# Attention scores as half-height matmuls: both components side by side in the array, three products each, one PSUM tile

## The chip, the cores and the metric

The kernel runs on one core of one Trainium2 chip. A core has a matrix engine (TensorE, "PE" in the profile), three others that compute (VectorE "DVE", ScalarE "ACT", GpSimd "POOL") and a queue engine (SyncE, "SP") that here issues nearly all DMAs. TensorE multiplies a stationary operand of up to 128 rows by 128 columns, loaded by a separate instruction ("PEld"), with a moving operand of up to 512 columns, and adds up in PSUM, a memory of eight banks of 512 float32 values per partition. The metric is the time of one execution on the device in microseconds (us).

## The reference

A decoder block of 2048 positions and 1024 channels: a normalised input is projected, one branch is a gated linear recurrence, the other a differential attention; both are gated, merged, projected and added to the input. The change is in the attention. Each of the 8 heads has two components (`c`) of 64 channels; each component gives scores and a softmax of its own, and the difference of the two, with a factor, weights the values.

```python
HEAD_DIM = D_MODEL // (2 * N_HEADS)          # 64
...
for qb in range(S // Q_BLOCK):               # 16 blocks of 128 queries
    ...
    s = jnp.einsum('bqhcd,bkhcd->bhcqk', q[:, q0:q1], k[:, :q1]).astype(jnp.float32) * scale
    ...
    p = jax.nn.softmax(s, axis=-1)
    w = p[:, :, 0] - lam * p[:, :, 1]
    outs.append(jnp.einsum('bhqk,bkhe->bqhe', w.astype(v.dtype), v[:, :q1]))
```

## The kernel before

**Numbers as pairs.** Nearly every float32 operand of a matmul is kept as a pair of float16 tiles, a high part and a low part (the rest). A product of two pairs is mostly taken as three matmuls, high x high, high x low and low x high.

**Stages.** From the start to about 468 us the recurrence branch runs. From 468 to about 1945 us runs the attention stage, in which the change lies. After it come the branch projections, the merge and the output projection.

**Attention units.** A unit is one head and 128 queries (`u.h`, `u.t`), 8 x 16 = 128 units in all. Unit t has t + 1 key blocks of 128 keys. `pieces(t)` (line 796) divides them into a first piece of at most eight blocks and, from t = 8 on, a second with the rest. `a_scores(u, ci)` (line 800) makes the scores of component `ci`, piece by piece: for each piece a PSUM tile `sc` of two banks (1024 columns) from the pool `ps_s` with two buffers (line 592), matmuls for each chunk of 512 keys (line 814), then VectorE copies the scores into an SBUF tile `e0` (component 0) or `e1` (component 1) and takes the row maximum (line 826), with the causal mask on the last block (line 830). The pool of `e0` and `e1` has four buffers each.

**The stacking before.** Component `ci` has 64 channels, half of the array's rows. K is therefore stored as `[128, 2, 512]`: for each component the high part on partitions 0 to 63 and the low part on 64 to 127. Q is stored twice per component, once high over low (`v = 0`) and once low over high (`v = 1`). Two matmuls over all 128 rows then give all four products:

```python
for v in range(2):
    nc.tensor.matmul(ps[:, x * 128:x * 128 + m], Qt[h, t // 4][:, v, ci, q0:q0 + 128],
                     K[:, ci, 0:m], start=(v == 0), stop=(v == 1))
```

**How K and Q get there.** The projections `g_k` and `g_q` (lines 672 and 685) make 128 channels of a head for 512 positions, component 0 on partitions 0 to 63 and component 1 on 64 to 127, by 24 matmuls (`mm3`, line 192). `split16` (line 665) writes the high part with ScalarE (line 667) and the low part with VectorE (line 668) into a tile `st`; DMAs on SP then move the halves into place, four for K (lines 680 and 681) and six for Q (lines 693 to 695). They are put off (`later`) until the next projection group has been issued.

**The rest of a unit.** `a_exp` (line 837) applies the exponential on ScalarE (line 851). `a_comb` (line 854) combines both components on VectorE (line 874), takes the high part on ScalarE (876) and the low part on GpSimd (877), and transposes both by DMA (880) into `pt`. `a_pv` (line 886) multiplies with v (line 897).

**Order.** The string `ORD = "0fc1eFp"` gives the order within a unit: the scores of component 0 ("0"), one group of projections ("f"), the combination of the unit before ("c"), the scores of component 1 ("1"), the exponentials ("e"), the other projection groups that are due ("F"), and the product with v of two units earlier ("p"). Projection groups are those for k, q, v with its gate (`g_va`, line 711) and the merge gates (`g_gm`). A planner of the framework may move instructions of an engine from this order when their inputs or buffers would not be ready.

Of the kernel before, what the change touches and what calls it, by code (L numbers as in the profile page):

```python
# [24 lines left out]
CH = 512  # L25
NC = S // CH
HALF = 1024
EPS = 1e-6
GM_T = 8   # groups of gate projections kept for the end of the attention
LAG = 2    # units between a unit's scores and its product with v  # L30
ACC0 = 8.0  # projection groups ahead of the attention units
PD = 5     # x tiles loaded ahead
# order in an attention unit: scores (0, 1), exponentials (e), combination of the unit before (c),
# product with v of an earlier one (p), with projection groups between them (f: one, F: all that are due)
ORD = "0fc1eFp"
SEG_A = 2  # where a head's gate projections stand between its chunks
SEG_B = 5
# [6 lines left out]
def p2(e):  # L44
    return float(2.0 ** e)
# [3 lines left out]
def kernel(  # L49
# [44 lines left out]
    with ExitStack():  # L94
# [33 lines left out]

# [1 line left out]
        class W:  # L130
            pass

        def w16_at(i):
            """one of the four places for a block of weights"""
            return lambda w: w16_p.tile([128, 2, KD, 128], F16, tag=f"w{i % 4}", name="w16")
# [24 lines left out]
        def w_scale(w, ps, fac, keep=None):  # L160
            """power of two that brings the block's norm close to 2^13 (a rough sum is enough for it)"""
            nc.tensor.matmul(ps[:, 0:1], ones16, w.ss, start=True, stop=True)
            tot = tl(1, "w_tot")
            nc.vector.tensor_scalar(out=tot, in0=ps[:, 0:1], scalar1=1e-30, scalar2=None, op0=ALU.max)
            w.sg, w.iv = keep or (tl(1, f"w_sg_{w.tag}"), tl(1, f"w_iv_{w.tag}"))
            pow2_bits(w.sg, tot, 13)
            pow2_inv(w.iv, w.sg)
            if keep is None:
                w.cz = wn_p.tile([128, 1], F32, tag=f"w_cz_{w.tag}", name="w_cz",
                                 bufs={"wg": 4, "agm": 3}.get(w.tag, 2))  # L170
                nc.vector.scalar_tensor_tensor(out=w.cz, in0=w.iv, scalar=fac, in1=cu, op0=ALU.mult, op1=ALU.mult)
# [9 lines left out]

# [1 line left out]
        utx = ExitStack()  # L183
# [3 lines left out]
        def mm3(ps, w, c0, n):  # L187
            """ps[f128, n] += w^T u over all of d, s in [c0, c0 + n)"""
            i = 0
            for k in range(KD):  # L190
                for a, b in ((0, 0), (0, 1), (1, 0)):
                    nc.tensor.matmul(ps, w.t[:, a, k, :], uT[:, b, k, c0:c0 + n],  # L192
                                     start=(i == 0), stop=(i == 3 * KD - 1))
                    i += 1

        # ================= RG-LRU branch =================
        with ExitStack() as lx:
# [21 lines left out]
            def prep_g(gr):  # L219
                """power of two that keeps the scaled, normalised input in fp16's range"""  # L220
                ss, tot = tl(1, "g_ss"), tl(1, "w_tot")
# [56 lines left out]

            # weight pipeline
            order = [(C_XR if i % 2 == 0 else C_ZR) + (i // 2) * 128 for i in range(2 * KD)]  # L280
# [16 lines left out]
            def in_half(b, hf, z, w):  # L297
                """PSUM tile of a half row of an x_r (z = 0) or z_r (z = 1) block"""
                if hf == 0 and 2 * b + z < 3:
# [142 lines left out]
            x_fin(4, 2, gb)  # L442
            # per-channel vectors: rows of 128 channels, turned into columns
            rows = le.tile([65, 128], F32, tag="rows", bufs=1, name="rows")
# [24 lines left out]
            with tc.issue_after(x_last[1]):  # L469
                # block-diagonal gate weights, exact f32r hi/lo  # L470
                gf_t = []
# [13 lines left out]
            with after_x():  # L485
                nc.vector.tensor_scalar(out=ba, in0=ba, scalar1=0.5, scalar2=None, op0=ALU.mult)
                nc.vector.tensor_scalar(out=bx, in0=bx, scalar1=0.5, scalar2=None, op0=ALU.mult)
                # softplus(-a) = max(-a, 0) + log1p(exp(-|a|)), log1p(t) = 2 atanh(t / (2 + t))
                spm, spe, sps, spq, spr = (lc.tile([128, KD], F32, name=f"sp{i}") for i in range(5))
# [85 lines left out]

        # ================= differential attention and merge gates =================
        QT = S // 128
        wfac_a = cst.tile([128, KD], F32, name="wfac_a")
        ya_ss = cst.tile([128, NH * NC], F32, name="ya_ss")
        with ExitStack() as ax:  # L580
# [10 lines left out]
            t4 = ax.enter_context(tc.tile_pool(name="t4", bufs=6))  # L591
            ps_s = ax.enter_context(tc.tile_pool(name="ps_s", bufs=2, space=PSUM))
            ps_o = ax.enter_context(tc.tile_pool(name="ps_o", bufs=2, space=PSUM))
            ps_m = ax.enter_context(tc.tile_pool(name="ps_m", bufs=2, space=PSUM))

# [1 line left out]
            wl = {k: ws[2 * KD + i] for i, k in enumerate(ahead)}  # L597
# [16 lines left out]
            def wadv(n):  # L614
                """weight blocks up to index n ready; two more on their way"""
                while wpos[0] < min(n + 3, len(worder)) or wpos[1] < min(n + 2, len(worder)) or wpos[2] < min(n + 1, len(worder)):
# [38 lines left out]

# [1 line left out]
            Kt, Qt, Vt, Gt = {}, {}, {}, {}  # L657
# [6 lines left out]

            def split16(ps):
                st = sp.tile([128, 2, CH], F16, tag="st", name="st")
                nc.scalar.activation(st[:, 0], ps, AF.Copy, scale=p2(-14))
                nc.vector.scalar_tensor_tensor(out=st[:, 1], in0=ps, scalar=p2(-14), in1=st[:, 0],  # L668
                                               op0=ALU.mult, op1=ALU.subtract)
                return st  # L670

            def g_k(h, c):
                ps = ps_m.tile([128, CH], F32, tag="mm", name="mm")
                mm3(ps, wl["k", h], c * CH, CH)
                st = split16(ps)
                t = kp.tile([128, 2, CH], F16, tag="K", name="K")

                def mv():
                    for i in range(2):
                        nc.sync.dma_start(out=t[0:64, i, :], in_=st[64 * i:64 * i + 64, 0, :])  # L680
                        nc.sync.dma_start(out=t[64:128, i, :], in_=st[64 * i:64 * i + 64, 1, :])
                later.append(mv)
                Kt[h, c] = t

            def g_q(h, c):
                ps = ps_m.tile([128, CH], F32, tag="mm", name="mm")
                mm3(ps, wl["q", h], c * CH, CH)
                st = split16(ps)
                t = qp.tile([128, 2, 2, CH], F16, tag="Q", name="Q")

                def mv():
                    for i in range(2):
                        nc.sync.dma_start(out=t[0:64, :, i, :], in_=st[64 * i:64 * i + 64, :, :])
                        nc.sync.dma_start(out=t[64:128, 0, i, :], in_=st[64 * i:64 * i + 64, 1, :])
                        nc.sync.dma_start(out=t[64:128, 1, i, :], in_=st[64 * i:64 * i + 64, 0, :])
                later.append(mv)
                Qt[h, c] = t
# [93 lines left out]

# [1 line left out]
            class U:  # L793
# [5 lines left out]

            def a_scores(u, ci):  # L800
                h, t = u.h, u.t
                if ci == 0:
                    u.n = 1 if t == 0 else (2 if t <= 8 else 3)
                    u.mx = t4.tile([128, 2, 3], F32, tag="mx", name="mx")
                    u.e = {}
                col = 0
                for pi, (b0, nb) in enumerate(pieces(t)):
                    ps = ps_s.tile([128, 1024], F32, tag="sc", name="sc")
                    for x in range(0, nb, 4):
                        m = min(4, nb - x) * 128  # L810
                        K = Kt[h, (b0 + x) // 4]
                        q0 = (t % 4) * 128
                        for v in range(2):
                            nc.tensor.matmul(ps[:, x * 128:x * 128 + m], Qt[h, t // 4][:, v, ci, q0:q0 + 128],  # L814
                                             K[:, ci, 0:m], start=(v == 0), stop=(v == 1))
                    if ci == 0:
# [5 lines left out]
                    u.e[ci, pi] = (e, ev)  # L822
                    last = b0 + nb == t + 1
                    m = (nb - 1 if last else nb) * 128
                    if m:
# [3 lines left out]
                    if last:  # L829
                        nc.vector.tensor_tensor_reduce(out=ev[:, m:m + 128], in0=ps[:, m:m + 128], in1=mask,  # L830
                                                       op0=ALU.add, op1=ALU.max, scale=1.0, scalar=-3e38,
                                                       accum_out=u.mx[:, ci, col:col + 1])
                        col += 1

# [138 lines left out]

        # ================= branch projections, merge, output projection =================
        with ExitStack() as bx_:
# [178 lines left out]

            # norm of the attention branch's rows, for a bound on the merged sum
            ya_n = bs.tile([128, 1], F32, name="ya_n")
# [52 lines left out]
```

## Time and profile before

| | |
|---|---|
| median of 3 runs | 2501.16 us (2499.86 to 2504.77) |
| span of the profiled execution | 2506.1 us |
| attention stage | 468 to 1945 us |
| busy in the attention stage: TensorE, VectorE, ScalarE, GpSimd | 1406, 980, 834, 360 us of 1477 |
| score matmuls (line 814) | 1280, busy 287.2 us |
| moves of K and Q by DMA | 128 and 192 |

Times of single instructions come from one profiled execution; its own time is its span, which is 4.9 us above the median of the unprofiled runs. A line of the view by groups has the kernel's line, the engine, the operation, what it writes and reads, the shape and the count, then the busy time in us (time in which at least one of the group ran), the mean length of one in ns, and the idle time of the engine in front of them with what ended it. Matmuls overlap: the next one streams while results of the one before still leave the array, so the busy time of a group over its count is less than the length of one.

### The profile page before, as it was taken

To read this page: it belongs to the slowest core of one execution; us is meant where nothing else is said; L and a number is where in the kernel's file an instruction comes from. 1 tells how busy PE (TensorE), PEld (TensorE's weight loads), DVE (VectorE), ACT (ScalarE), POOL (GpSimd) and SP (SyncE) were. 2 spreads that over 40 slices of the span, in tenths; PEclk is the share of its full clock that TensorE was granted. 3 is DMA by queue.
4 is the path that set the end of the run, shared out by engine and by line. 5 is a ranking of instruction groups with operands and counts; after the bars stand their busy time and mean duration, and the time that the engine had idled before them with its cause. 6 is when DMAs were issued, how large, how long until landed. Compare 5 with 4: busy or idle time off the path is not lost. (4 is left out here: it accounts for less than half of the span.)

```text
span 2506.1 us, 41430 instructions
## 1 busy us (share of the span) xinstructions
PE 2353.1 (94%) x15240; PEld 1355.3 (54%) x15240; DVE 1548.4 (62%) x4316; ACT 1224.6 (49%) x2156; POOL 679.7 (27%) x415
## 2 busy tenths in 40 slices
PE   6789999999998999998998999999999899999998
PEld 5344444465665665665665655655655444444443
DVE  8877667668658566667567478468467244633323
ACT  5555545456547546556456457356456244312211
POOL 3443334212222212222222222223123133322211
PEclk9899999999999999999999999999999999999999
DMA  9511111235444534635535445445445854743202
GB/s 244 104 43 48 46 42 34 76 81 119 108 96 111 113 84 108 127 82 113 115 84 114 103 96 118 95 90 124 95 90 115 251 177 135 239 148 118 84 17 101
DMA packets 541323, 268.73 MB, mean 107 GB/s; under 512 B 370504, under 2 KB 518016, under 8 KB 541120
## 3 DMA queue, kind: packets, MB, share of 16 engines
q1 hardware_dynamic: 538144, 256.74, 42.6%
q0 software_dynamic: 2816, 9.08, 1.2%
q8 instruction: 119, 1.95, 0.3%
q14 instruction: 84, 0.69, 0.1%
q10 hardware_dynamic: 160, 0.27, 0.0%
HBM read 110.79 MB, written 41.94 MB: 61 GB/s over the span
## 5 line engine op out<-in xcount | busy, mean ns | idle before, releaser
L192 PEld LDWEIGHTS <-w 128*128 128x128 f16 x5040 | 475.9, 100 | 576.5 <-issue 89.2
L192 PE MATMUL mm<-uT,w 128*128 128x512 f16 x3072 | 705.1, 383 | 12.9 <-ACT gm L728 8.9
L877 POOL TENSOR_TENSOR e<-e,e 128x1024 f16<-128x1024 f32 (+2 forms) x192 | 317.0, 1666 | 970.6 <-ACT e L876 487.0
L851 ACT ACTIVATE e<-e,nb,sc_h 128x1024 f32<-128x1024 f32 (+7 forms) x384 | 376.1, 980 | 160.8 <-DVE nb L845 125.6
L826 DVE TENSOR_SCALAR_CACHE_REDUCE e<-sc 128x1024 f32<-128x1024 f32 (+7 forms) x352 | 305.2, 880 | 134.9 <-PE sc L814 122.3
L192 PE MATMUL ps<-uT,w 128*128 128x512 f16 (+1 forms) x1968 | 354.4, 345 | 26.1 <-ACT xr L318 17.7
L711 PE MATMUL mm<-wva,uT 128*128 128x256 f16 x3072 | 352.7, 275 | 3.3 <-DVE st L668 2.6
L1094 PE MATMUL psb<-yt,w 128*128 128x512 f16 x1536 | 332.9, 379 | 2.0 <-ACT w L177 1.5
L711 PEld LDWEIGHTS <-uT 128*128 128x128 f16 x3072 | 301.5, 99 | 48.8 <-issue 2.9
L814 PE MATMUL sc<-K,Q 128*128 128x512 f16 (+3 forms) x1280 | 287.2, 351 | 19.9 <-DVE e L826 13.8
L897 PE MATMUL o<-V,pt 128*128 128x128 f16 x3264 | 224.5, 222 | 38.4 <-DMA pt<-e 38.1
L1094 PEld LDWEIGHTS <-w 128*128 128x128 f16 x1536 | 149.1, 98 | 184.9 <-issue 3.9
L897 PEld LDWEIGHTS <-pt 128*128 128x128 f16 x3264 | 200.0, 99 | 72.8 <-DMA pt<-e 46.5
L876 ACT ACTIVATE e<-e 128x1024 f16<-128x1024 f32 (+2 forms) x192 | 150.1, 802 | 143.1 <-DVE e L874 118.5
L814 PEld LDWEIGHTS <-Q 128*128 128x128 f16 x1280 | 119.6, 99 | 133.2 <-issue 20.2
L874 DVE SCALAR_TENSOR_TENSOR e<-e,rs,e 128x1024 f32<-128x1024 f32 (+2 forms) x192 | 190.0, 1017 | 2.2
L1125 PE MATMUL psf<-wo,m 128*128 128x512 f16 x720 | 155.7, 379 | 0.0
L156 ACT ACTIVATE jk<-wst 128x1024 bf16<-128x1024 f32 x80 | 84.2, 1052 | 138.7 <-DMA wst<-in_w_in_dram 102.6
L1125 PEld LDWEIGHTS <-m 128*128 128x128 f16 x768 | 75.1, 98 | 90.6
L1098 DVE SCALAR_TENSOR_TENSOR t<-gt,psb 128x512 f32<-128x512 f32 x64 | 43.8, 686 | 120.2 <-PE psb L1094 100.1
L1148 ACT ACTIVATE jk<-psf 128x1024 bf16<-128x1024 f32 x15 | 15.4, 1024 | 134.0 <-PE psf L1125 69.4
L717 DVE SCALAR_TENSOR_TENSOR V<-mm,V 128x256 f16<-128x256 f32 x64 | 26.9, 421 | 85.7 <-ACT V L716 85.6
(247 smaller groups left out, 2417.3 us busy)
## 6 DMA issues: line engine op xcount, KB each, us to landing
wst<-in_w_in_dram SPq DMA_DIRECT2D x64, 512.0 KB, 4.5
xt<-in_x_dram SPq DMA_DIRECT2D x32, 512.0 KB, 4.5
gm_d<-gm SPq DMA_DIRECT2D x64, 256.0 KB, 2.7
gt<-gm_d SPq DMA_DIRECT2D x32, 512.0 KB, 3.8
K<-st SPq DMA_DIRECT2D x128, 64.0 KB, 2.0
Q<-st SPq DMA_DIRECT2D x64, 128.0 KB, 2.4
Q<-st SPq DMA_DIRECT2D x128, 64.0 KB, 2.1
ya_d<-yT SPq DMA_DIRECT2D x64, 128.0 KB, 2.0
```

Source lines behind the costliest of these rows:

```text
L156: nc.scalar.activation(jk, w.st, AF.Square, accum_out=ss)
L192: nc.tensor.matmul(ps, w.t[:, a, k, :], uT[:, b, k, c0:c0 + n], start=(i == 0), stop=(i == 3 * KD - 1))
L711: nc.tensor.matmul(ps[:, j, :], uT[:, a, k, s0:s0 + 128], wt[:, b, k].rearrange("p t f -> p (t f)"), start=(i == 0), stop=(i == 3 * KD - 1))
L814: nc.tensor.matmul(ps[:, x * 128:x * 128 + m], Qt[h, t // 4][:, v, ci, q0:q0 + 128], K[:, ci, 0:m], start=(v == 0), stop=(v == 1))
L826: nc.vector.tensor_scalar(out=ev[:, 0:m], in0=ps[:, 0:m], scalar1=1.0, scalar2=None, op0=ALU.mult, op1=ALU.max, accum_out=u.mx[:, ci, col: ...
L851: nc.scalar.activation(ev[:, 0:nb * 128], ev[:, 0:nb * 128], AF.Exp, bias=nb_[:, ci:ci + 1], scale=sc_h[h], accum_out=u.sm[:, pi, ci:ci + 1])
L874: nc.vector.scalar_tensor_tensor(out=e0[:, 0:m], in0=e1v[:, 0:m], scalar=rs, in1=e0[:, 0:m], op0=ALU.mult, op1=ALU.add)
L876: nc.scalar.activation(e1[:, 0, 0:m], e0[:, 0:m], AF.Copy)
L877: nc.gpsimd.tensor_tensor(out=e1[:, 1, 0:m], in0=e0[:, 0:m], in1=e1[:, 0, 0:m], op=ALU.subtract)
L897: nc.tensor.matmul(o, pt[:, a, kb % 8, :], V[:, kb % 4, b, :], start=(kb == 0 and i == 0), stop=(kb == n - 1 and i == 2))
L1094: nc.tensor.matmul(ps, w.t[:, p, k, :], y_t[b][:, q, k, sl], start=(i == 0), stop=(i == 3 * KD - 1))
L1125: nc.tensor.matmul(pn[n], m16[:, a, j, ms], wo[:, b, j, ns], start=(j == 0 and a == 0 and b == 0), stop=(j == KD - 1 and a == 1))
```

## The change

- `split16` writes the high and low parts straight into the K or Q tile. Both tiles are now `[128, 2, 512]`, high and low, with component 0 on partitions 0 to 63 and component 1 on 64 to 127, as the projection leaves them. The tile `st` and the DMAs of K and Q are gone.
- `a_scores` takes a piece (`pi`) in place of a component: "0" in the order string now means the first piece of both components, "1" the second piece, which units below t = 8 don't have.
- The scores of a piece go into one PSUM tile of four banks, two per component, from a pool with one buffer.
- Each component takes three products of 64 rows each (high x high, high x low, low x high), the two components in turn.
- The copies into `e0` and `e1` follow for both components of the piece.

Comments are taken out throughout; that part of the diff is left out here.

```diff
-            ps_s = ax.enter_context(tc.tile_pool(name="ps_s", bufs=2, space=PSUM))
+            ps_s = ax.enter_context(tc.tile_pool(name="ps_s", bufs=1, space=PSUM))
...
-            def split16(ps):
-                st = sp.tile([128, 2, CH], F16, tag="st", name="st")
-                nc.scalar.activation(st[:, 0], ps, AF.Copy, scale=p2(-14))
-                nc.vector.scalar_tensor_tensor(out=st[:, 1], in0=ps, scalar=p2(-14), in1=st[:, 0],
+            def split16(ps, t):
+                nc.scalar.activation(t[:, 0], ps, AF.Copy, scale=p2(-14))
+                nc.vector.scalar_tensor_tensor(out=t[:, 1], in0=ps, scalar=p2(-14), in1=t[:, 0],
                                                op0=ALU.mult, op1=ALU.subtract)
-                return st
...
-                st = split16(ps)
                 t = kp.tile([128, 2, CH], F16, tag="K", name="K")
-
-                def mv():
-                    for i in range(2):
-                        nc.sync.dma_start(out=t[0:64, i, :], in_=st[64 * i:64 * i + 64, 0, :])
-                        nc.sync.dma_start(out=t[64:128, i, :], in_=st[64 * i:64 * i + 64, 1, :])
-                later.append(mv)
+                split16(ps, t)
                 Kt[h, c] = t
...
-                st = split16(ps)
-                t = qp.tile([128, 2, 2, CH], F16, tag="Q", name="Q")
-
-                def mv():
-                    for i in range(2):
-                        nc.sync.dma_start(out=t[0:64, :, i, :], in_=st[64 * i:64 * i + 64, :, :])
-                        nc.sync.dma_start(out=t[64:128, 0, i, :], in_=st[64 * i:64 * i + 64, 1, :])
-                        nc.sync.dma_start(out=t[64:128, 1, i, :], in_=st[64 * i:64 * i + 64, 0, :])
-                later.append(mv)
+                t = qp.tile([128, 2, CH], F16, tag="Q", name="Q")
+                split16(ps, t)
                 Qt[h, c] = t
...
-            def a_scores(u, ci):
+            def a_scores(u, pi):
+
                 h, t = u.h, u.t
-                if ci == 0:
+                if pi == 0:
...
-                col = 0
-                for pi, (b0, nb) in enumerate(pieces(t)):
-                    ps = ps_s.tile([128, 1024], F32, tag="sc", name="sc")
-                    for x in range(0, nb, 4):
-                        m = min(4, nb - x) * 128
-                        K = Kt[h, (b0 + x) // 4]
-                        q0 = (t % 4) * 128
-                        for v in range(2):
-                            nc.tensor.matmul(ps[:, x * 128:x * 128 + m], Qt[h, t // 4][:, v, ci, q0:q0 + 128],
-                                             K[:, ci, 0:m], start=(v == 0), stop=(v == 1))
+                if pi >= len(pieces(t)):
+                    return
+                b0, nb = pieces(t)[pi]
+                pss = ps_s.tile([128, 2, 1024], F32, tag="sc", name="sc")
+                q0 = (t % 4) * 128
+                Q = Qt[h, t // 4]
+                for x in range(0, nb, 4):
+                    m = min(4, nb - x) * 128
+                    K = Kt[h, (b0 + x) // 4]
+                    for i, (a, b) in enumerate(((0, 0), (0, 1), (1, 0))):
+                        for ci in range(2):
+                            r = slice(64 * ci, 64 * ci + 64)
+                            nc.tensor.matmul(pss[:, ci, x * 128:x * 128 + m], Q[r, a, q0:q0 + 128], K[r, b, 0:m],
+                                             start=(i == 0), stop=(i == 2))
+                last = b0 + nb == t + 1
+                m = (nb - 1 if last else nb) * 128
+                for ci in range(2):
+                    ps = pss[:, ci]
                     if ci == 0:
                         e = ep.tile([128, 1024], F32, tag="e0", name="e0")
                         ev = e
...
                     u.e[ci, pi] = (e, ev)
-                    last = b0 + nb == t + 1
-                    m = (nb - 1 if last else nb) * 128
+                    col = pi
                     if m:
```

More of the change, by code (lines that the diff above doesn't have):

```diff
@@ L832, in a_scores @@
                                                        accum_out=u.mx[:, ci, col:col + 1])
-                        col += 1
             s0_t = {}
```

## The prediction

> **What bounds the kernel now.** I read the page first (sections 1 and 2), then the busy time by stage, then the groups of TensorE by shape in the attention stage, then its timeline and its waits.
>
> ```profile
> span 2506.1 us, 41430 instructions
> PE 2353.1 (94%) x15240; PEld 1355.3 (54%) x15240; DVE 1548.4 (62%) x4316; ACT 1224.6 (49%) x2156; POOL 679.7 (27%) x415
> PE   6789999999998999998998999999999899999998
> PEclk9899999999999999999999999999999999999999
> ```
>
> TensorE is the bound: 94% busy, near its ceiling in almost every slice, at the full clock after the first few. The next engine, VectorE, is at 62%. The profiled execution spans 2506.1 us; the median of the three runs is 2501.16 us, 4.9 us (0.2%) less. All terms below are differences made in the profiled execution, and I set them on the median. The three runs lie between 2499.86 and 2504.77 us, 0.2% apart, so 0.2% (5 us) is what I count as a change.
>
> The score matmuls stand only in the attention stage, from 468 to 1945 us (columns: length, then busy time and count of each engine).
>
> ```profile
> core 0: us, PE busy (x) PEld busy (x) DVE busy (x) ACT busy (x) POOL busy (x), PEclk, DMA share, GB/s
> 468.00:1945.00 1477.00, 1406.08 (x10494) 891.97 (x10494) 979.81 (x3235) 833.97 (x1690) 359.95 (x227) 0.98 0.49 104
> ```
>
> TensorE is idle there for 1477.0 - 1406.1 = 71 us, VectorE for 497. A microsecond less of matmuls is therefore worth nearly a microsecond, as long as nothing that TensorE waits for becomes later. Its groups in this stage, by shape, and from the last stage the densest group of the kernel:
>
> ```profile
> L192 PE MATMUL mm<-uT,w 128*128 128x512 f16 x2881 | 660.9, 382 | 5.3 <-DVE w_tot L164 3.8 <-ACT gm L728 1.4
> L711 PE MATMUL mm<-wva,uT 128*128 128x256 f16 x3072 | 352.7, 275 | 3.3 <-DVE st L668 2.6 <-ACT wva L177 0.6
> L814 PE MATMUL sc<-K,Q 128*128 128x512 f16 x896 | 237.4, 384 | 15.6 <-DVE e L826 13.8 <-DVE mx L830 1.6
> L897 PE MATMUL o<-V,pt 128*128 128x128 f16 x3216 | 221.5, 222 | 38.4 <-DMA pt<-e 38.1
> L814 PE MATMUL sc<-K,Q 128*128 128x384 f16 x128 | 31.5, 332 | 0.6 <-DVE mx L830 0.5
> L814 PE MATMUL sc<-K,Q 128*128 128x256 f16 x128 | 23.8, 272 | 0.2
> L814 PE MATMUL sc<-K,Q 128*128 128x128 f16 x128 | 17.5, 219 | 3.5 <-DMA Q<-st 3.0 <-issue 0.3 <-PE sc L814 0.2
> ```
>
> ```profile
> L1125 PE MATMUL psf<-wo,m 128*128 128x512 f16 x720 | 155.7, 379 | 0.0
> ```
>
> A matmul's place in the stream is the group's busy time over its count, since records overlap: 155.7 / 720 = 216 ns for 512 columns, though one record lasts 379 ns. The other 163 ns are the tail, in which its results still leave the array while the next one streams. In the same way 256 columns take 352.7 / 3072 = 115 ns and 128 columns 221.5 / 3216 = 69 ns; 384 columns I put between, at 165. The score groups themselves read higher per matmul because each short run of them counts a tail, so I price them with these rates.
>
> **Part 1, the products.** Before, each 512-key chunk of a component takes two matmuls over all 128 rows, four per chunk for both components: 896 x 0.216 + 128 x 0.165 + 128 x 0.115 + 128 x 0.069 = 238 us. Afterwards a chunk takes six matmuls, three on rows 0 to 63 (component 0) and three on rows 64 to 127 (component 1), alternating, each component into its own banks. No row of this trace shows two matmuls side by side on halves of the array. The bounds are that a pair takes the place of one matmul, or of two. As one: three places where there were four, 672 x 0.216 + 96 x 0.165 = 161 us for the wide ones, and for the two narrow shapes 192 places that I take at two loads and two matmuls, 2 x 0.069 = 0.138 us, 26.5 us. Together 187.5 us: **51 us less**. As two: 1344 x 0.216 + 192 x (0.165 + 0.115 + 0.069) = 357 us: 119 us more. I take the first, since the two use different rows, different moving data and different banks, and nothing they share is visible in the trace.
>
> The Trainium skill, "TensorE: Matmul & The Clock Gate", section "Part 3: Packing small matmuls — row/col tiling", says that matmuls on different row groups run together and start about 4 ns apart. By that my estimate for the pairs would be 960 x 4 ns = 4 us longer, a gain of 47 us instead of 51.
>
> **Part 2, changes of the array's shape.** A score piece (up to eight key blocks, both components) is now a run of half-height matmuls between full-height ones. There are 16 + 8 pieces per head, 192 in all, so 384 changes, in and out. This timeline shows the surroundings of a piece (start, length, engine, line, operation):
>
> ```profile
> 1701.34 0.17 PE L162 MATMUL tot<-w_s,ones 128*128 128x1 bf16 x1
> 1701.37 1.57 PE L814 MATMUL sc<-K,Q 128*128 128x512 f16 x8
> 1702.77 0.28 PE L897 MATMUL o<-V,pt 128*128 128x128 f16 x2
> 1702.88 5.40 PE L711 MATMUL mm<-wva,uT 128*128 128x256 f16 x48
> 1708.12 1.57 PE L814 MATMUL sc<-K,Q 128*128 128x512 f16 x8
> 1709.53 1.89 PE L897 MATMUL o<-V,pt 128*128 128x128 f16 x31
> ```
>
> Between shapes of full height a change costs nothing today: the run of eight at 1701.37 starts 0.03 us behind the one-column matmul, and the product with v starts at 1702.77 while the last score record runs to 1702.94. That is the lower bound, 0 per change; it cannot be a gain, since nothing is removed at a change. What the trace cannot show is whether a half-height matmul may enter while a full-height one is still leaving. If not, the tail of 163 ns is laid open at each change. If the weight load has to wait as well, its length comes on top:
>
> ```profile
> L814 PEld LDWEIGHTS <-Q 128*128 128x128 f16 x1280 | 119.6, 99 | 133.2 <-issue 20.2 <-DVE mx L830 4.0 <-DMA Q<-st 3.1
> ```
>
> 163 + 99 = 262 ns, the upper bound. So the term lies between 0 and 384 x 0.262 = 101 us. [...]
>
> The Trainium skill, "TensorEngine Tiling (Array Packing)", section "Key Properties", says that changing the tiling mode, though not the tile, drains TensorE. It gives no price. No run here shows it yet; by that rule the bottom of my bounds is excluded, and without it the sum would be 63 us lower.
>
> **Part 3, one score tile of four banks in place of two of two.** The next piece may start only when VectorE has copied both components of the piece before. Its rows in this stage, the copy of 1024 columns, the masked block, and the read of the row maximum behind a copy:
>
> ```profile
> L826 DVE TENSOR_SCALAR_CACHE_REDUCE e<-sc 128x1024 f32<-128x1024 f32 x128 | 156.2, 1220 | 90.3 <-PE sc L814 80.5 <-PE tot L162 4.6 <-POOL e L877 4.1
> L830 DVE CUSTOM_DVE_ANT_0 e<-sc,mask 128x128 f32<-128x128 f32 x256 | 72.7, 286 | 10.2 <-PE sc L814 7.6 <-PE tot L162 2.5
> L826 DVE DVE_READ_ACCUMULATOR e<-sc 128x1 f32 x352 | 29.1, 83 | 0.0
> ```
>
> A full piece needs 2 x (1.22 + 0.08) = 2.6 us of copying behind its last matmul. Between a unit's two pieces stands a projection group, 5.2 us in the timeline above (1702.88 to 1708.12), which covers it; between the second piece and the next unit's first stands the product with v (1.9 us and more), which covers it less well. If the cover is gone, a piece waits for up to 2.6 us, and everything behind it on TensorE waits too, projections included. The copies also come earlier for component 1, in front of the combination of the unit before instead of behind it, and their target is one of four buffers that are freed by GpSimd and then two transposing DMAs:
>
> ```profile
> L877 POOL TENSOR_TENSOR e<-e,e 128x1024 f16<-128x1024 f32 (+2 forms) x192 | 317.0, 1666 | 970.6 <-ACT e L876 487.0
> L880 SPq DMA_TRANSPOSE pt<-e x384: 1102/1238/2972, 510.4 to 1952.6; - x192
> ```
>
> That is 1.7 + 2 x 1.2 us at least, in a unit of 1477 / 128 = 11.5 us. The waits of TensorE in this stage:
>
> ```profile
> PE o L897 <- DMA pt<-e: 38.1, 30, 3.2
> PE sc L814 <- DVE e L826: 13.8, 9, 4.4
> PE sc L814 <- DMA Q<-st: 3.0, 5, 1.2
> PE sc L814 <- DVE mx L830: 2.1, 3, 1.3
> ```
>
> Scores wait 13.8 + 2.1 = 16 us for copies now. With both components in one tile I take twice that, **16 us more**; the bounds are 0 and one copy (1.3 us) at each of the 64 second pieces, 83 us.
>
> **Part 4, the moves that go.** The K and Q halves are written in place; the DMAs that rearranged them fall away (lines as min/median/max in ns):
>
> ```profile
> L680 SPq DMA_DIRECT2D K<-st x64: 461/583/1195, 468.2 to 1870.5; - x64
> L681 SPq DMA_DIRECT2D K<-st x64: 461/587/1462, 473.2 to 1871.8; - x64
> L693 SPq DMA_DIRECT2D Q<-st x64: 616/628/1307, 485.4 to 1883.6; - x64
> L694 SPq DMA_DIRECT2D Q<-st x64: 467/602/1612, 486.1 to 1884.2; - x64
> L695 SPq DMA_DIRECT2D Q<-st x64: 461/592/1382, 486.8 to 1880.8; - x64
> ```
>
> 320 issues at 0.6 us free SP for 190 us, against 384 x 1.24 = 475 us that the transposes need on the same queue. What TensorE feels of it are the 3.0 us on Q and some of the 38.1 us on the transposes; since those mostly follow a late combination and not a full queue, I count 5 of the 38: **8 us less**, between 3 and 41. ScalarE and VectorE keep the same two instructions per split; they write straight into a K or Q tile whose last readers, earlier score matmuls, stand before the projection on TensorE anyway, so no wait is added (cover: TensorE's own order; should it fail, one split, below 2 us per group).
>
> **Sum**: -51 + 63 + 16 - 8 = +20 us: 2501 + 20 = **2521 us**, slower by 0.8%. Without the changes of shape it would be -43, so the price that decides is 43 / 384 = 0.11 us per change.
>
> **Rivals.** *Free changes of shape* (the other side): in each of the 192 pieces the half-height matmuls follow the full-height ones with no gap; price 0, decided below 0.11 us per change. For it speaks that the trace shows no gap at any change of width, against it that no change of height is among them. -43 us: 2458 us. *The halves do not run together*: +119 in place of -51, with free changes of shape, 119 + 16 - 8 = +127: 2628 us, and 63 more with dear ones. For it: the trace never shows two matmuls in the array side by side; against it: nothing common to the two halves shows either. The change would then not do what it says. *The single score tile becomes the bound*: the 64 second pieces each wait for a copy, -51 + 83 - 8 = +24 with free changes: 2525 us. For it speak the existing 16 us; against it the 5.2 us of projections that stand between.
>
> **How the numbers follow.** My forecast (dear changes, from just above the deciding price to the upper bound: -43 + 101 = +58) has 0.46, its own range is 2506 to 2559 us. Changes that are free or below 0.11 us have 0.42, from 2458 us up. Halves that don't run together have 0.08, the score tile as the bound 0.04. The range takes in the first two and the last, with the free case's copies hidden altogether (-51 - 8 = -59, 2442 us) and some 10 us of extra waiting above the dear one: 2442 to 2568 us; the halves one after the other stay outside. Within 0.2%: 0.09, prices near the deciding one, 0.06 from the forecast and 0.03 from the free case. Faster by over 0.2%: 0.42 - 0.03 = 0.39. Slower by over 0.2%: 0.46 - 0.06 + 0.08 + 0.04 = 0.52.
>
> **What would show it.** In the new profile the score matmuls number 1920; the stream of a wide pair should advance by about 216 ns. If the halves run one after the other, it advances by 432. In front of the first half-height matmul of a piece and behind its last one a gap of some 0.16 us in TensorE's stream should stand; none would make me wrong to the fast side. Waits of the scores on the copies should read near 32 us instead of 16, those on the transposes near 33, and the moves of K and Q are gone. I am wrong in the size if waits on copies pass 60 us.

## The result and the profile after

The changed kernel takes 2546.26 us (median of four runs, 2542.68 to 2551.34) against 2501.81 us for the kernel before (also four runs; the median above is of three): ratio 1.0175, 95% interval 1.0157 to 1.0193, 44 us slower. The forecast was 20 us slower: right in sign, inside the range, less than half of the size.

The profiled execution spans 2540.9 us against 2506.1 before, so the two profiles hold 35 of the 44 us. The head of its page, then its stage row (length, then busy time and count by engine; until 1985 us, since the attention stage now ends later: its last product with v starts at 1992.6 us instead of 1956.9):

```profile
span 2540.9 us, 42053 instructions
PE 2339.1 (92%) x15880; PEld 1304.3 (51%) x15880; DVE 1544.0 (61%) x4316; ACT 1227.2 (48%) x2156; POOL 669.0 (26%) x415
```

```profile
468.00:1985.00 1517.00, 1399.05 (x11183) 843.02 (x11182) 982.15 (x3237) 839.18 (x1693) 356.40 (x229) 0.98 0.41 86
```

TensorE has 640 more matmuls and is nevertheless busy 14 us less over the whole span; it now stands idle for 118 us of 1517 where it stood idle for 71 of 1477. The score matmuls as one group of the page, then by shape beside the same dense group as before:

```profile
L804 PE MATMUL sc<-K,Q 64*128 64x512 f16 (+3 forms) x1920 | 216.4, 353 | 34.4 <-DVE e L819 21.8
```

```profile
L804 PE MATMUL sc<-K,Q 64*128 64x512 f16 x1344 | 175.2, 386 | 28.9 <-DVE e L819 19.6 <-DVE s L859 4.2 <-DVE mx L823 4.1
L1117 PE MATMUL psf<-wo,m 128*128 128x512 f16 x720 | 155.7, 379 | 0.0
...
L804 PE MATMUL sc<-K,Q 64*128 64x384 f16 x192 | 22.2, 331 | 3.0 <-DVE w_iv_agm L115 1.6 <-DVE mx L823 1.0 <-DVE e L819 0.2
...
L804 PE MATMUL sc<-K,Q 64*128 64x256 f16 x192 | 15.9, 271 | 1.9 <-DVE e L819 1.9
...
L804 PE MATMUL sc<-K,Q 64*128 64x128 f16 x192 | 11.1, 221 | 0.7 <-ACT Q L666 0.7
```

All score matmuls together (line 804) are busy for 216 us, where those of line 814 were for 287. The two halves do run together. One piece in the timeline (start, length, operation):

```profile
1505.83 1.00 PE L889 MATMUL o<-V,pt 128*128 128x128 f16 x15
1506.76 1.47 PE L804 MATMUL sc<-K,Q 64*128 64x512 f16 x12
1508.16 0.45 PE L889 MATMUL o<-V,pt 128*128 128x128 f16 x5
```

Twelve matmuls of 512 columns in 1.47 us are six places of 216 ns and a tail; the second of a pair starts 3 ns (median) behind the first. Pairs of 384, 256 and 128 columns advance by 163, 109 and 56 ns. By the mean spacing of the two traces the stream of the scores is 56 us shorter, 179 us instead of 235. Both ends show the change of shape: from the start of a full-height matmul to the start of the half-height one behind it, the trace has 96 ns more than the width alone takes (median of 155 changes that no wait disturbs, nine tenths of them between 95 and 96), and 92 ns more on the way out (178 changes). With some 390 changes that is 37 us.

The waits of TensorE in the stage, then those of VectorE, and behind them VectorE's in the kernel before, which were not shown there:

```profile
PE o L889 <- DMA pt<-e: 60.8, 38, 5.5
PE sc L804 <- DVE e L819: 21.8, 18, 3.6
...
PE sc L804 <- DVE mx L823: 5.1, 9, 1.0
PE sc L804 <- DVE s L859: 4.2, 2, 2.2
```

```profile
DVE s L854 <- ACT e L843: 171.6, 53, 6.1
...
DVE s L859 <- ACT e L843: 48.5, 58, 1.9
...
DVE rs L858 <- ACT e L843: 26.8, 46, 1.0
```

```profile
DVE s L862 <- ACT e L851: 83.0, 39, 5.1
...
DVE s L867 <- ACT e L851: 32.1, 41, 1.5
...
DVE rs L866 <- ACT e L851: 18.4, 40, 1.0
```

So the pairs came as reckoned, and the changes of shape were cheaper than reckoned. What grew are the waits. The product with v waits 61 us for transposes (38 before), the scores 31 us for VectorE (16 before), and VectorE stands 247 us at the head of the combination, waiting for exponentials, where it stood 133.

### The profile page after: what moved, and what is told of

Same layout as the page of the kernel before. It is cut to its first block, busy times and chain, and to the rows that moved or that the text cites. A ratio compares the mean times of both kernels' runs of the same rounds, so it can differ in the third digit from the quotient of the medians.

```text
span 2540.9 us, 42053 instructions
## 1 busy us (share of the span) xinstructions
PE 2339.1 (92%) x15880; PEld 1304.3 (51%) x15880; DVE 1544.0 (61%) x4316; ACT 1227.2 (48%) x2156; POOL 669.0 (26%) x415
## 5 line engine op out<-in xcount | busy, mean ns | idle before, releaser
L869 POOL TENSOR_TENSOR e<-e,e 128x1024 f16<-128x1024 f32 (+2 forms) x192 | 310.9, 1633 | 980.1 <-ACT e L868 567.1
L804 PE MATMUL sc<-K,Q 64*128 64x512 f16 (+3 forms) x1920 | 216.4, 353 | 34.4 <-DVE e L819 21.8
L804 PEld LDWEIGHTS <-Q 64*128 64x128 f16 x1920 | 77.9, 95 | 143.0 <-DVE e L819 32.1
L854 DVE TENSOR_TENSOR s<-sm 128x2 f32<-128x2 f32 x64 | 10.2, 160 | 171.6 <-ACT e L843 171.6
L823 DVE CUSTOM_DVE_ANT_0 e<-sc,mask 128x128 f32<-128x128 f32 x256 | 72.0, 285 | 27.0 <-PE sc L804 25.7
```

The costliest lines, as they stand in the source:

```text
L804: nc.tensor.matmul(pss[:, ci, x * 128:x * 128 + m], Q[r, a, q0:q0 + 128], K[r, b, 0:m], start=(i == 0), stop=(i == 2))
L869: nc.gpsimd.tensor_tensor(out=e1[:, 1, 0:m], in0=e0[:, 0:m], in1=e1[:, 0, 0:m], op=ALU.subtract)
```

## The experiments

All ratios are to the kernel before on the same chip, with 95% intervals. Comments in the cuts from the diffs name the run. First question: where do the waits come from? Three theories: A, the score tile that comes free only as a whole; B, the order by pieces; C, the changes of shape, dearer than the spacing shows.

**old_rows_new_order**: full height, stacked K and Q and all moves as before, but order and tile of the changed kernel (the cut is against the changed kernel).

```diff
-                    for i, (a, b) in enumerate(((0, 0), (0, 1), (1, 0))):
+                    for v in range(2):
                         for ci in range(2):
-                            r = slice(64 * ci, 64 * ci + 64)
-                            nc.tensor.matmul(pss[:, ci, x * 128:x * 128 + m], Q[r, a, q0:q0 + 128], K[r, b, 0:m],
-                                             start=(i == 0), stop=(i == 2))
+                            nc.tensor.matmul(pss[:, ci, x * 128:x * 128 + m], Q[:, v, ci, q0:q0 + 128], K[:, ci, 0:m],
+                                             start=(v == 0), stop=(v == 1))
```

> The kernel before with its stacked K and Q, its DMAs and its two full-height products, but in the order of the changed kernel: pieces instead of components, one score tile of four banks with one buffer. Theories A and B (the loss is in tile and order): slower than before by the waits alone, 2501.8 plus 30 to 60 us, 2530 to 2560 us. Theory C (shape changes are the loss): as before, 2500 to 2510 us.

Measured: 1.0186 (1.0160 to 1.0212), 2555.49 us. With no half-height matmul at all the loss is as large as in the changed kernel; order and tile alone cost some 47 us here, so theory C alone can't be it. That the two losses are equal is chance, as moves_back will show. TensorE's waits:

```profile
PE o L903 <- DMA pt<-e: 54.4, 34, 4.2
PE sc L818 <- DVE e L833: 13.6, 10, 3.5
PE sc L818 <- DVE mx L837: 9.0, 6, 4.6
```

**old_rows_pieces_two_tiles**: the same with `bufs=2` and a tile of two banks per component.

> The kernel before (stacked rows, DMAs, full-height products) in the order by pieces, but with its two score tiles of two banks. The same kernel with one tile of four banks ran at 1.0186 of before. If the order by pieces is what costs (theory B), still 1.014 to 1.020, 2536 to 2552 us. If the one tile costs (theory A), 1.000 to 1.006, 2502 to 2517 us.

Measured: 1.0081 (1.0064 to 1.0099). The order costs about 20 us and the single tile another 26, so A and B each hold a part.

**old_order_one_tile**: the kernel before with one tile of four banks for a component's two pieces, `pss = ps_s.tile([128, 2, 1024], ...)`, `bufs=1`.

> The kernel before in its own order by components, but with one score tile of four banks and one buffer for both pieces of a component. Theory A (one tile): 1.010 to 1.020 of before, 2527 to 2552 us. Theory B (order): 0.998 to 1.005, 2497 to 2515 us.

Measured: 1.1021 (1.1002 to 1.1040), 2760 us, far beyond what was expected. Every component now waits until the one before has been copied:

```profile
DVE e L827 <- PE sc L815: 286.5, 160, 6.1
```

VectorE waits for scores, TensorE for copies, by turns. With a single tile, the order by pieces is by far the better one.

**comp_tiles**: the changed kernel with a tile of two banks per component, from a pool with two buffers.

```diff
-                pss = ps_s.tile([128, 2, 1024], F32, tag="sc", name="sc")
+                pss = [ps_s.tile([128, 1024], F32, tag="sc", name="sc") for _ in range(2)]
```

> The changed kernel with one PSUM tile of two banks per component (two buffers) in place of one of four banks: the matmuls and their order stay. Theory A (the loss is waiting for the copies of a score tile that is given back only as a whole): component 0's banks come free one copy earlier, so about half of the added waits go, 2515 to 2530 us. Theory B (the loss is the order by pieces, which puts both components' copies in front of the combination and the maxima behind it): unchanged within 5 us, 2541 to 2551 us. Theory C (the loss is the array's changes of shape, dearer than the 0.09 us that the spacing of the matmuls shows): unchanged as well.

Measured: 1.0265 (1.0244 to 1.0286), slower, as no theory had it. The planner, free to use each tile as it came free, drew the two components apart:

```profile
1501.81 0.82 PE L696 MATMUL mm<-wva,uT 128*128 128x256 f16 x6
1502.56 1.47 PE L804 MATMUL sc<-K,Q 64*128 64x512 f16 x6
1503.96 0.28 PE L696 MATMUL mm<-wva,uT 128*128 128x256 f16 x1
1504.08 0.22 PE L889 MATMUL o<-V,pt 128*128 128x128 f16 x1
1504.23 1.47 PE L804 MATMUL sc<-K,Q 64*128 64x512 f16 x6
```

Six matmuls of one half take the 1.47 us that twelve of both took. In the trace 543 of the 960 pairs still start together, against 957 in the changed kernel, and there are 140 changes of shape more. By the rates above I estimate some 90 us more of stream (417 more places and the changes) for 23 us more of time; the waits for transposes fell to 12 us meanwhile. In the changed kernel the shared tile keeps the pairs together. The run mixes these effects and doesn't decide between A and B.

**halves_in_turn**: in each chunk the three products of component 0, then the three of component 1 (the two inner loops exchanged).

> The changed kernel with the three products of component 0 first and then the three of component 1 in each chunk, nothing else changed. If the halves run together only where neighbours in the queue lie on different halves, a chunk takes five places or, across chunks, four in place of three: 60 to 125 us more, 2605 to 2670 us. If the array fetched ahead far enough to pair them anyhow, 2546 us.

Measured: 1.0180 (1.0160 to 1.0200), as the changed kernel. The built program has the order 0 0 0 1 1 1 0 0 0 1 1 1 (read there; the trace doesn't name the half of a matmul), and yet twelve matmuls take 1.47 us, six places, with the two of a pair starting some 10 ns apart:

```profile
1513.55 1.47 PE L804 MATMUL sc<-K,Q 64*128 64x512 f16 x12
```

With that order, a matmul of the second half starts ahead of earlier ones in the queue that wait for the first half. In queue order nine places would be the least.

**chunk_tiles** has a tile per 512 keys for both components, with two buffers, and copies per tile; **lag3** has the product with v three units behind; **chunk_lag3** has both; **e_5** has five buffers for the copied scores.

```diff
-                pss = ps_s.tile([128, 2, 1024], F32, tag="sc", name="sc")     # chunk_tiles, in the loop over x
+                    pss = ps_s.tile([128, 2, 512], F32, tag="sc", name="sc")
...
-LAG = 2                                                                       # lag3
+LAG = 3
-            tp = ax.enter_context(tc.tile_pool(name="tp", bufs=4))
+            tp = ax.enter_context(tc.tile_pool(name="tp", bufs=6))
...
-            ep = ax.enter_context(tc.tile_pool(name="ep", bufs=4))            # e_5
+            ep = ax.enter_context(tc.tile_pool(name="ep", bufs=5))
```

> The changed kernel with a score tile per chunk of 512 keys (both components, two banks, two buffers): a chunk's copies run while the next chunk's matmuls do, and VectorE copies 512 columns at a time (0.68 us instead of half of 1.22). Theory A: the waits of the scores for the copies fall by two thirds, 2505 to 2525 us in spite of some 15 us more copying. Theory B: 2540 to 2560 us. Theory C: 2540 to 2555 us or more, if more runs of half-height matmuls arise.

> The changed kernel with the product with v three units behind the scores instead of two, and six buffers for the transposed weights instead of four (the space comes from the Q tiles and the tile for the moves, which are gone). TensorE waits 64 us for transposes in the changed kernel. If these waits are a loss of their own, they nearly vanish: 2490 to 2510 us. If they only stand in for waits further up the chain (exponentials, copies), the time is lost elsewhere: 2535 to 2550 us.

> Both changes that could shorten waits together, on the changed kernel: a score tile per 512 keys with two buffers, and the product with v three units behind with six buffers. Alone they ran at 1.0178 and 1.0117. If the waits for copies and those for transposes are separate losses, 1.010 to 1.013. If finer tiles only helped once the product with v no longer waits, below 1.008; below 1.000 it would beat both kernels.

> The changed kernel with five instead of four buffers for the copied scores of each component. Component 1's copies now come in front of the combination of the unit before, and their buffers come free only after two transposes. If that is what VectorE stands behind, 1.008 to 1.013. VectorE is seen to wait only 6 us for transposes in the changed kernel; if that is all, 1.015 to 1.018.

Measured: 1.0178 (1.0157 to 1.0198), 1.0117 (1.0102 to 1.0132), 1.0217 (1.0198 to 1.0237) and 1.0167 (1.0145 to 1.0189). Only the longer distance helps, by 0.006, which lies between its two expectations. In lag3 the waits for transposes halve, and some of that comes back at the scores:

```profile
PE sc L804 <- DVE e L819: 30.3, 16, 7.9
PE o L889 <- DMA pt<-e: 29.0, 20, 3.1
```

In chunk_lag3, which was slower than any of its expectations, the waits for transposes nearly vanish (2.5 us) and those of the scores take their place:

```profile
PE sc L809 <- DVE e L819: 55.5, 41, 5.4
```

Finer tiles did not help as theory A had it. The buffers of the copied scores are not the cause.

**comb_last** (`ORD = "0f1ceFp"`):

> The changed kernel with the combination of the unit before put behind the second pieces' scores instead of in front of them. In the changed kernel VectorE stands 247 us at the head of the combination waiting for exponentials, against 133 us before, and the copies of the second pieces queue behind it. If that queueing is the loss, the score waits of TensorE fall by half and the time to 2515 to 2530 us. If the combination comes too late for the transposes instead, 2545 to 2560 us.

Measured: 1.0181 (1.0159 to 1.0204). The planner made the same order of instructions from it on every engine, so it doesn't test the question; it is the changed kernel once more.

**moves_back**: the tile `st` and ten DMAs per chunk of K and Q put back, with the half-height products. For K:

```diff
-                split16(ps, t)
+                st = split16(ps)
+                def mv():
+                    for i in range(2):
+                        nc.sync.dma_start(out=t[64 * i:64 * i + 64, 0, :], in_=st[64 * i:64 * i + 64, 0, :])
+                        nc.sync.dma_start(out=t[64 * i:64 * i + 64, 1, :], in_=st[64 * i:64 * i + 64, 1, :])
+                later.append(mv)
```

> The changed kernel with the tile for the halves and the DMAs of K and Q put back (four and six per chunk, same sizes and the same places in the queue order as before; they now copy to where the halves would have been written anyway, and the Q tile has a second copy that nothing reads). The changed kernel ran at 1.0175 of before. The prediction took 8 us for the moves, between 3 and 41: 1.019 to 1.033, most likely 1.021. If the freed queue is worth nothing, because the waits for transposes come from a late combination, 1.016 to 1.019.

Measured: 1.0281 (1.0254 to 1.0308). Taking the moves away was worth 27 us, more than three times what was forecast. It also means that half-height products with the moves kept (1.0281) are slower than full-height ones in the same arrangement (1.0186).

Second question: what is the shorter stream worth? **more_changes** has 256 further changes of shape in the changed kernel. **before_three_places** and **old_rows_three_places** leave out component 1's second product. **old_rows_with_changes** has 384 changes of shape in old_rows_new_order.

```diff
+                    if x:                                                     # more_changes
+                        nc.tensor.matmul(pss[:, 0, x * 128:x * 128 + 1], ones16, ones16[:, 0:1], start=True, stop=True)
...
-                        for v in range(2):                                    # before_three_places
+                        for v in range(2 - ci):
...
-                    for v in range(2):                                        # old_rows_three_places
-                        for ci in range(2):
+                    for v, ci in ((0, 0), (0, 1), (1, 0)):
...
+                nc.tensor.matmul(pss[:, 0, 0:1], Q[0:64, 0, 0, q0:q0 + 128], Kt[h, b0 // 4][0:64, 0, 0:1],
+                                 start=True, stop=True)                       # old_rows_with_changes
```

> The changed kernel with a full-height matmul of one column (ones by ones, into a place that the next chunk's first product overwrites) in front of every second chunk of a piece: 128 of them, 256 further changes of the array's shape. At 0.094 us per change, as the spacing in the changed kernel shows, and 0.03 us for the column itself, 256 x 0.094 + 128 x 0.03 = 28 us more if TensorE's stream sets the time: 1.027 to 1.030. At the 0.163 us of the prediction 46 us: 1.036. If the stage is set by the chain of copies, exponentials and transposes, so that TensorE has room between, 5 to 15 us: 1.019 to 1.024.

> The kernel before, leaving out component 1's second product in each chunk: 58 us less of matmuls, everything else as it was. The prediction took a microsecond of matmuls for nearly a microsecond of time: 0.977 to 0.981. If freed time turns into waiting here too, 0.985 to 0.998.

> The full-height kernel in the order by pieces with one score tile (1.0186 of before), leaving out component 1's second product, so that each chunk takes three places in TensorE's stream instead of four, as the pairs do, and no change of shape. Stream shorter by 58 us. If TensorE's stream sets the time here, 1.0186 - 0.023: 0.995 to 1.000. If the chain of copies, exponentials and combination sets it, so that freed time turns into waiting, 1.010 to 1.019.

> The same full-height kernel with all its products, and a half-height matmul of one column in front of each piece (its place is overwritten by the piece's first product): 192 of them, 384 changes of shape, as many as in the changed kernel. Spacing alone: 384 x 0.094 + 192 x 0.03 = 42 us, 1.034 to 1.037. If TensorE has room between its waits, less: 1.022 to 1.030. If changes cost more than the spacing shows, above 1.040.

Measured: 1.0244 (1.0215 to 1.0272), 17 us for 28 us of stream. 1.0009 (0.9997 to 1.0021): **58 us of matmuls less in the kernel before were worth nothing.** 1.0043 (1.0030 to 1.0057) against 1.0186: 36 us for 58. 1.0279 (1.0262 to 1.0297) against 1.0186: 23 us for 42. Changes of shape thus cost less time than the spacing shows, not more, and theory C falls. The stage row and the waits of before_three_places:

```profile
468.00:1945.00 1477.00, 1362.49 (x10141) 867.07 (x10140) 991.62 (x3231) 833.10 (x1689) 355.33 (x227) 0.97 0.49 103
```

```profile
PE o L897 <- DMA pt<-e: 58.3, 43, 4.7
PE sc L814 <- DVE e L826: 20.4, 14, 3.5
PE tot L162 <- DVE w_s L158: 17.5, 4, 10.5
```

In the same 1477 us TensorE is idle for 115 us instead of 71: 44 us of the freed time went into waits, above all for transposes (58 instead of 38), copies (20 instead of 14) and weight sums (18 instead of 4). Most of the rest went into a lower clock, which I had overlooked (0.97 in the row instead of 0.98): in this stage the trace has TensorE at half the clock for 96 us instead of 51, and matmuls of 512 columns start 427 ns apart there instead of 216. By that spacing I estimate 12 us more of streaming. The planner also made another order here: the combination stands between the copies of the two components in 28 units instead of 43 (counted as in the table further down). So what is shown is that the time doesn't follow the matmuls, not that nothing else changed.

Third question, since half height with the moves kept came out slower although its stream is shorter: does it cost anything more, or does the planner's order differ? **moves_back_acc9**, **old_rows_acc9** and **before_acc9** change only the number of projection groups ahead (`ACC0 = 9.0`).

> moves_back (1.0281) with one projection group more ahead of the attention units; the work is the same, its order is not. If half-height products carry a cost of their own, within 0.004 of moves_back: 1.024 to 1.032. If the order made the difference, it comes nearer to the sum of the parts, 1.011 to 1.020.

> old_rows_new_order (1.0186) with one projection group more ahead. If orders of the same work differ little, 1.015 to 1.022. If they differ by more than 10 us, outside of that on either side.

> The kernel before with one projection group more ahead, no other change. If orders of the same work differ little, 0.997 to 1.004. If the order matters by more than 10 us, outside of that, and slower is likelier, since 8 groups is the setting the kernel before has.

Measured: 1.0225 (1.0207 to 1.0243), 1.0114 (1.0099 to 1.0129), 1.0042 (1.0030 to 1.0054). Another order of the same work moves the time by 10 to 18 us, and moves_back_acc9 fell between its two expectations. The distance between half height and full height stays, though: 0.0095 with one order, 0.0111 with the other. The price of order and tile at full height does not stay: it is 46 us with 8 groups ahead (1.0186 against 1) and 18 us with 9 (1.0114 against 1.0042). None of the versions beats the kernel before.

## Why the prediction was wrong in size

Step by step, in ratios times 2501.8 us, each step uncertain by the 10 to 18 us that an order alone can make: the order by pieces +20, the one tile +26, half height with the moves kept +24, the moves taken away -27. The steps lie one behind the other, from the kernel before to the changed one, so it is no test of them that they add up to the measured 44 us (43 after rounding). Against the forecast's terms:

| | forecast | runs |
|---|---|---|
| Parts 1 and 2, half height | -51 + 63 = +12 us | +24 us |
| Part 3, order and tile | +16 us | +46 us |
| Part 4, moves | -8 us | -27 us |

Two steps failed: the claim that ties time to TensorE's stream, on which Parts 1 and 2 rest, and the size of Part 3. Part 4 was mis-sized as well.

**The first claim fell**, "A microsecond less of matmuls is therefore worth nearly a microsecond". The condition that I attached to it, as long as nothing that TensorE waits for becomes later, was the point. Before_three_places shows it: 58 us less of matmuls became 44 us more of waits and, by the estimate above, 12 us of slower streaming. The share of 94% busy gave no hint of that. The stream of Part 1 did get shorter, by 56 us instead of 51, since the narrow pairs took 109 and 56 ns instead of the 138 that I put down. By this run such a gain is worth nothing in the old arrangement, and by old_rows_three_places about 0.6 of it at full height in the new one.

**Part 2 was too dear.** 63 us were put down, 384 changes at the whole tail of 0.163 us. No run shows that term: the spacing shows 0.092 to 0.096 us per change, 37 us, inside the bounds and 0.6 of the tail. The Trainium skill, "TensorEngine Tiling (Array Packing)", section "Key Properties", says that a change of the tiling mode drains TensorE, and gives no price; the trace agrees in so far as every undisturbed change shows a gap, of 0.09 us. By the measured price the forecast's own sum would have been 2495 us, on the wrong side. The right sign was luck: the error in Part 2 covered the others.

**Part 3 failed most in size**: 16 us against 20 + 26 = 46 on the full-height kernel. I took twice the scores' waits for copies and looked only at the wait that carries the tile's name. In the profile of old_rows_new_order the scores wait 23 us for copies instead of 16, but the product with v waits 54 us for transposes instead of 38, and VectorE stands 189 us at the head of the combination instead of 133. The rival that stood nearest was the single score tile as the bound, though it too put the waits at the scores alone. With one projection group more ahead the same difference is 18 us, close to the forecast, so the 46 us belong to this order as well as to the tile.

**Part 4 was too small**: 27 us instead of 8, inside its bounds. The waits for transposes stand at 61 us where 33 were expected, but the moves are not to blame: moves_back shows 73 us for them with the moves in place, so taking these away saved 12 us there.

```profile
PE o L905 <- DMA pt<-e: 72.7, 46, 6.5
```

**Half height costs 24 us although its stream is 19 us shorter (-56 + 37).** With one projection group more ahead it is 28 us. The waits for transposes grow with it, from 54 us in old_rows_new_order to 73 in moves_back, and from 36 to 49 with the other order. What the traces show besides is VectorE's order. Of the 64 units of two pieces, 56 follow another one of two pieces; counted is where the first step of the combination stands among the unit's copies:

```
                     between the halves of the copies   ahead of all copies   elsewhere
before                              43                          7                 6
old_rows_new_order                  29                         26                 1
moves_back                          16                         40                 0
changed kernel                      16                         40                 0
```

In the changed kernel the combination of the unit before, which waits for exponentials, mostly stands in front of all the unit's copies; that goes with the 247 us that VectorE waits there. No run undid this order, so it stays argued, and so does the reason for which the planner orders half-height products in this way. The cause of the 24 us is open.

The rivals: free changes of shape did not come about, nor halves that run one after the other (except in comp_tiles, where the planner parted them).

## What to carry to other kernels

A busy share of 94% doesn't say that less work is less time: leave a part of the work out and see whether the time falls, before reckoning a saving. Count the buffers that an arrangement frees together: one tile of four banks in place of two of two cost 26 us in one order of the work and 255 us in another, and the price appeared at other names than the tile's. Where a planner makes the order, two orders of the same work lay 10 to 18 us apart here, so a change of 1% has to be told from that too.

## What the runs showed of the hardware

Two half-height matmuls on different rows and banks ran in the place of one (six places for twelve matmuls, starts 3 ns apart), for which the Trainium skill, "TensorE: Matmul & The Clock Gate", section "Part 3: Packing small matmuls — row/col tiling", gives about 4 ns. The same section of the Trainium skill has matmuls start in strict queue order; halves_in_turn shows pairs (starts 10 ns apart) out of a built program in which three matmuls of one half stand ahead of three of the other, and the measurement decides. A change between full and half height costs 0.092 to 0.096 us of TensorE's stream, and the weight load waits with it: at both ends of the piece shown above the first load starts 4 ns ahead of its matmul, where loads of full-height matmuls otherwise start about one place ahead (54 to 215 ns).
